# A two-layer trunk step on one core: the end of the first mixer in one written TensorE order, and a constant load later in the queue

## The chip, the core and the metric

The program runs on one core of a Trainium2 chip. The metric is the device time of one execution in microseconds; the median of several runs counts. The engines are TensorE (PE, with its weight loads shown as PEld), VectorE (DVE), ScalarE (ACT), GpSimd (POOL) and SyncE (SP), which here only issues the transfers from and to the device's memory. Each engine works through its own list of instructions in order; semaphores tie the lists together.

## The reference

Two token streams of 128 rows each (a prompt and a sample with cached context) pass through two layers of width 2048. Each layer modulates its input with shift, scale and gate (six vectors from `silu(cond) @ w_ada`), runs a mixer, adds the result, modulates again and runs a gated feed-forward part with a width-3 convolution. The first layer's mixer is the one that the change touches:

```python
def mixer_ab(h, rope, ctx, w_in, g_q, w_q_up, g_kv, w_kv_up, g_qn, g_kn, w_out):
    proj = h @ w_in
    ...
    qa = (rmsnorm(q_lat, g_q) @ w_q_up).reshape(b, t, MLA_HEADS, MLA_NOPE_DIM + MLA_ROPE_DIM)
    ...
    kv = (ckv_all @ w_kv_up).reshape(b, s, MLA_HEADS, MLA_NOPE_DIM + MLA_V_DIM)
    ...
    out_a = softmax_attention(jnp.concatenate([qa_nope, qa_rope], axis=-1), ka, va, MLA_SCALE)
    out_b = softmax_attention(qb, kb_all, vb_all, HEAD_SCALE)
    out = jnp.concatenate([out_a.reshape(b, t, -1), out_b.reshape(b, t, -1)], axis=-1) @ w_out
    return out, new_ctx
```

Eight latent heads (A) and eight grouped heads (B) give 16 x 128 features, and `w_out` (2048 x 2048) projects them.

## The kernel before

Activations lie with features on the 128 partitions: chunk `k` holds features 128k to 128k+127 of the 256 tokens. A matrix product is done in three passes per 128 x 128 block, so that nearly the full precision of 32-bit numbers is kept: each weight tile `raw` is split into a high part `wh` (ScalarE, line 247) and the remainder `wl` (VectorE, line 248), the operand likewise, and TensorE adds wh x high, wh x low and wl x high. A chunk of 128 output features over 16 input blocks is 48 matmuls into one PSUM bank `acc`. The `raw` tiles (1 MB) come over SyncE into three buffers, `wh` and `wl` have four buffers of eight blocks each.

Three kinds of side work run beside these products. `row_step` computes modulation vectors on TensorE from tiles `araw` (tiles `ada`, then a copy `am` on ScalarE, a transpose and a reduction on VectorE). `feature_step` and the class `Deep` compute others on VectorE: line 520 is one such sum of about 1.2 us over half a tile (`block`, `kvb` or `more`, 512 KB, one transfer for two sums), with a product that nobody reads written to a scratch place `junk`. `pump` spreads these steps over the program, and `step` moves on the chains (Python generators) that hold each head's attention.

The first mixer has two parts. In the first, `part` multiplies 23 chunks of `w_in_ab`, in stretches of the input features. Its TensorE order is written out: while `pe.in_turn` is set, each matmul passes `keep_order`, and an instruction that passes it stays behind all that were issued before it on its engine. A class `Feed` sets the order of its transfers; `late_constants` is one of them, 512 KB of constants (rope tables, biases beyond the first, gains) of which VectorE's first use is line 1331.

In the second part, the loop over `h` in 0, 2, 4, 6 makes the queries and keys of two latent heads, begins two grouped heads (`gqa`), makes the values (`values`) and begins the two latent heads (`mla_pair`). Each head goes: scores on TensorE, maxima on VectorE (lines 862 and 863), two small steps on GpSimd, exponentials on ScalarE (line 870), scaling of `p` on VectorE (lines 898 to 900), three transposes on TensorE (line 112, `att<-cst,p`), a copy `pT` on ScalarE, three products with the values, and the split of the result into operand `o` (`hx` in the profile). Chunk `h` of `o` is a latent head, chunk 8 + h a grouped one.

Then `out_ab` multiplies by `w_out`. Its first three chunks go through `first_three`, which names the order of the 48 pairs (chunk c, block k) in `PAIR_LATE`: for each chunk the blocks 8 to 15 (grouped heads), then 0 to 5, last 6 and 7 (the last pair). Here nothing is pinned, apart from one matmul in each pair's scores: a scheduler that works with its own estimates of time places the instructions, and it moves blocks of these three chunks in between the attention of the heads.

## Time and profile before

| | us |
|---|---|
| Median of 3 runs (lowest, highest) | 2307.14 (2306.03, 2307.19) |
| The profiled execution | 2304.7 |
| Its span, first to last instruction | 2302.9 |
| TensorE busy | 2272.1 (99%) |
| VectorE busy | 1886.1 (82%) |
| ScalarE busy | 1199.3 (52%) |
| Mean granted TensorE clock | 0.996 |

Rows of groups and of the timeline give: start in us, duration, engine, source line, operation, output tile <- inputs, shapes and how often; in square brackets the idle time of that engine just before and what ended it. Rows of a stage (a:b) give its length, then busy time (with instructions) of PE, PEld, DVE, ACT and POOL, the granted clock, the share of the transfer engines and GB/s. A matmul's duration in the timeline overlaps its neighbour's, so rates are read from the distance of the starts or from long runs.

### The profile page before, as it was taken

The page shows a single profiled execution, that of the slowest core. Times are in us where ns is not written, and L with a number is a line of the kernel's source. Part 1 is how long each engine was busy: PE and PEld are TensorE (multiplying, and loading weights), DVE is VectorE, ACT ScalarE, POOL GpSimd, SP SyncE. Part 2 cuts the span into 40 slices and gives each one's busy share as a digit, 9 for nine tenths or more (in the row PEclk, how much of TensorE's full clock was granted, in tenths as well). Part 3 has the DMA queues.
Part 4 walks back from the last instruction along what each step waited for, and adds up shares of the span by engine and source line. Part 5 has one row for each costly group of instructions (what it writes and reads, how often), then busy time and mean ns, then how long its engine had stood idle before and what let it go on. Part 6 is the DMA issues. An engine that isn't in the chain of part 4 may idle for free.

```text
span 2302.9 us, 47585 instructions
## 1 busy us (share of the span) xinstructions
PE 2272.1 (99%) x19528; PEld 2180.0 (95%) x19528; DVE 1886.1 (82%) x2973; ACT 1199.3 (52%) x1975; POOL 188.2 (8%) x238
## 2 busy tenths in 40 slices
PE   8899989999999999999999999999999999999998
PEld 6788868999999999999999999999999999999998
DVE  4668979889989999999988988898899965666654
ACT  4346555665554355555575455457555434555543
POOL 0012111300000000001130001023000000000011
PEclk9999999999999999999999999999999999999999
DMA  9988879777767777777787888776677755555553
GB/s 386 374 334 305 329 291 359 290 275 250 272 259 288 286 276 262 260 273 256 284 304 290 311 309 324 259 273 230 245 254 264 263 201 188 199 192 193 198 189 127
DMA packets 100122, 617.15 MB, mean 268 GB/s; under 512 B 10752, under 2 KB 18880, under 8 KB 33344
## 3 DMA queue, kind: packets, MB, share of 16 engines
q1 hardware_dynamic: 99904, 614.11, 72.0%
q8 instruction: 153, 2.51, 0.4%
q14 instruction: 65, 0.53, 0.1%
HBM read 609.32 MB, written 4.75 MB: 267 GB/s over the span
## 4 chain that ended last, share of the span: by engine, by line
PE 96%; DMA 2%; DVE 1%; ACT 1%; issue 0%; SPq 0%; POOL 0%; DVEq 0%; ACTq 0%; POOLq 0%
PE acc L109 89%; PE ada L109 3%; PE att L109 2%; PE att L112 1%; DMA raw<-w_in_ab 1%; DVE wl L248 1%; DMA kvb<-w_ada 0%; DMA araw<-w_ada 0%; PE misc L109 0%; ACT wh L247 0%; PE ada L112 0%; DVE hx L520 0%; DVE x L1616 0%; DVE qb L1138 0%; ACT p L870 0%
## 5 line engine op out<-in xcount | busy, mean ns | idle before, releaser
L109 PE MATMUL acc<-hx,wh 128*128 128x256 f32 (+1 forms) x7264 | 1252.4, 278 | 5.0 <-ACT wh L247 1.7
L247 ACT CAST wh<-raw 128x1024 fp32r<-128x1024 f32 (+1 forms) x834 | 796.6, 967 | 878.8 <-PE acc L109 745.7
L248 DVE TENSOR_TENSOR wl<-raw,wh 128x1024 fp32r<-128x1024 f32 (+1 forms) x834 | 924.4, 1124 | 248.2 <-ACT wh L247 243.3
L109 PEld LDWEIGHTS acc<-hx,wh 128*128 128x128 f32 x7264 | 1097.3, 188 | 23.8 <-issue 8.9
L109 PE MATMUL acc<-hx,wl 128*128 128x256 f32 (+1 forms) x3632 | 1005.7, 277 | 6.3 <-DVE wl L248 6.1
L109 PEld LDWEIGHTS acc<-hx,wl 128*128 128x128 f32 x3632 | 682.9, 188 | 10.5 <-DVE wl L248 7.9
L109 PE MATMUL acc<-g,wh 128*128 128x256 f32 x2816 | 478.8, 276 | 0.0
L109 PEld LDWEIGHTS acc<-g,wh 128*128 128x128 f32 x2816 | 423.8, 188 | 0.0
L109 PE MATMUL acc<-g,wl 128*128 128x256 f32 x1408 | 388.0, 276 | 0.0
L468 DVE CUSTOM_DVE_ANT_0 junk<-araw,condb 128x2048 f32<-128x2048 f32 x128 | 294.1, 2297 | 0.0
L109 PE MATMUL acc<-hxc,wh 128*128 128x256 f32 (+1 forms) x1568 | 282.7, 282 | 0.0
L109 PEld LDWEIGHTS acc<-g,wl 128*128 128x128 f32 x1408 | 264.1, 188 | 0.0
L109 PEld LDWEIGHTS acc<-hxc,wh 128*128 128x128 f32 x1568 | 241.3, 189 | 4.6 <-issue 4.2
L109 PE MATMUL acc<-hxc,wl 128*128 128x256 f32 (+1 forms) x784 | 218.4, 279 | 0.0
L210 POOL TENSOR_TENSOR sqacc<-sqacc,sq 128x256 f32<-128x256 f32 x62 | 71.5, 1154 | 1490.7 <-ACT sq L206 1490.4
L109 PEld LDWEIGHTS acc<-hxc,wl 128*128 128x128 f32 x784 | 147.5, 188 | 0.4
L1509 ACT ACTIVATE cv<-acc,convw 128x256 f32<-128x256 f32 x169 | 94.2, 558 | 0.0
L520 DVE CUSTOM_DVE_ANT_0 hx<-block,condb 128x1024 fp32r<-128x1024 f32 x65 | 79.2, 1218 | 7.4 <-DMA block<-w_ada 6.8
L1515 DVE SCALAR_TENSOR_TENSOR cv<-acc,convw,cv 128x254 f32<-128x254 f32 x169 | 80.8, 478 | 3.2
L838 DVE SCALAR_TENSOR_TENSOR x<-acc,mod,x 128x128 f32<-128x128 f32 x190 | 57.1, 342 | 31.7 <-PE acc L109 31.7
L1512 DVE SCALAR_TENSOR_TENSOR cv<-acc,convw,cv 128x254 f32<-128x254 f32 x169 | 80.1, 474 | 0.0
L109 PE MATMUL ada<-araw,condw 128*32 128x512 f32 (+1 forms) x608 | 75.7, 585 | 0.8 <-DMA araw<-w_ada 0.8
(263 smaller groups left out, 1532.9 us busy)
## 6 DMA issues: line engine op xcount, KB each, us to landing
raw<-w_up SPq DMA_DIRECT2D x176, 1024.0 KB, 4.8
araw<-w_ada SPq DMA_DIRECT2D x136, 1024.0 KB, 6.2
raw<-w_down SPq DMA_DIRECT2D x88, 1024.0 KB, 4.8
raw<-w_in_c SPq DMA_DIRECT2D x48, 1024.0 KB, 6.8
block<-w_ada SPq DMA_DIRECT2D x41, 512.0 KB, 6.6
raw<-w_in_ab SPq DMA_DIRECT2D x18, 1024.0 KB, 9.2
raw<-w_out_ab SPq DMA_DIRECT2D x16, 1024.0 KB, 8.2
raw<-w_out_c SPq DMA_DIRECT2D x16, 1024.0 KB, 6.5
```

Source lines behind the costliest of these rows:

```text
L109: return self.placed(nc.tensor.matmul(*a, **kw))
L112: return self.placed(nc.tensor.transpose(*a, **kw))
L210: eng.tensor_tensor(out=st["acc"], in0=st["acc"], in1=sq, op=ALU.add)
L247: pin(act.copy(out_hi, src))
L248: pin(dve.tensor_tensor(out=out_lo, in0=src, in1=out_hi.bitcast(F32), op=ALU.subtract))
L468: keep_order(dve.tensor_tensor_reduce(out=T_(feat["pool"], [P, D], "junk"), in1=feat["row"][:, c], in0=feat["raw"].rearrange("p g n -> p ( ...
L520: keep_order(dve.tensor_tensor_reduce(out=self.junk, in0=self.raw, in1=self.row[:, c].rearrange("p (g n) -> p g n", g=2), scale=1.0, scala ...
L838: dve.scalar_tensor_tensor(out=x[:, c, s], in0=ps[:, s], scalar=mod[:, l, 3 * which + 2, c, g:g + 1], in1=x[:, c, s], op0=ALU.mult, op1=AL ...
L1509: pin(act.activation(y, ps, AF.Identity, scale=cw[:, 1, m:m + 1], bias=cw[:, 3, m:m + 1]))
L1512: pin(dve.scalar_tensor_tensor(out=y3[:, :, 1:], in0=p3[:, :, :T - 1], scalar=cw[:, 0, m:m + 1], in1=y3[:, :, 1:], op0=ALU.mult, op1=ALU.add))
L1515: pin(dve.scalar_tensor_tensor(out=y3[:, :, :T - 1], in0=p3[:, :, 1:], scalar=cw[:, 2, m:m + 1], in1=y3[:, :, :T - 1], op0=ALU.mult, op1=A ...
```

## The change

`first_three` becomes a class `Three` that can be run in pieces; the function stays as a wrapper for the second mixer. In the loop's last turn (h == 6) the three chunks' weight tiles are requested and two of their halves prepared ahead of the values. From the last pair's scores on, `pe.in_turn` is set until the three chunks end: the scores, 20 blocks of the three chunks (60 matmuls), the transposes of both heads, 4 blocks, the products with the values, and the other 24 blocks. Three calls of `deep.pump` stand between the 20 blocks and one behind the 24th, with `junk` now in `qb`. The weight tile of the fourth chunk is requested there as well, and `out_ab` splits the fourth chunk's weights in two `W.ahead` steps behind the first two residuals. Apart from that, the constants go out behind the first tile of the third weight group (`rest`) instead of behind the second tile of the first one.

```diff
--- before.py
+++ after.py
@@ -329,26 +329,38 @@
             self.blocks = []
             return self.tiles[-1]
 
-    def first_three(W, xh, xl, order, mid=None, fixed=False, first=0):
-
-
-        pin = keep_order if fixed else lambda i: i
-        raws = [W.load()[0] for _ in range(3)]
-        ps = [T_(pacc, [P, 512], "acc") for _ in range(3)]
-        blocks = {(c, h): W.halves(raws[c], 8 * h) for c, h in ((0, first), (1, first), (2, first), (0, 1 - first))}
-        count = [0] * 3
-        for n, (c, k) in enumerate(order):
-            if mid and n == len(order) // 2:
-                mid()
-            if (c, k // 8) not in blocks:
-                blocks[c, k // 8] = W.halves(raws[c], k // 8 * 8)
-            wh, wl = blocks[c, k // 8][k % 8]
-            a, b = count[c] == 0, count[c] == KD - 1
-            count[c] += 1
-            pin(pe.matmul(ps[c][:, :NT], wh, xh(k), start=a, stop=False))
-            pin(pe.matmul(ps[c][:, :NT], wh, xl(k), start=False, stop=False))
-            pin(pe.matmul(ps[c][:, :NT], wl, xh(k), start=False, stop=b))
-        return [p[:, :NT] for p in ps]
+    class Three:
+
+        def __init__(self, W, xh, xl, order):
+            self.W, self.xh, self.xl, self.order = W, xh, xl, list(order)
+            self.raws = [W.load()[0] for _ in range(3)]
+            self.blocks, self.count, self.ps = {}, [0] * 3, []
+
+        def prepare(self, c, h):
+            self.blocks[c, h] = self.W.halves(self.raws[c], 8 * h)
+
+        def banks(self):
+            self.ps = [T_(pacc, [P, 512], "acc")[:, :NT] for _ in range(3)]
+
+        def run(self, n):
+            for _ in range(n):
+                c, k = self.order.pop(0)
+                if (c, k // 8) not in self.blocks:
+                    self.prepare(c, k // 8)
+                wh, wl = self.blocks[c, k // 8][k % 8]
+                a, b = self.count[c] == 0, self.count[c] == KD - 1
+                self.count[c] += 1
+                pe.matmul(self.ps[c], wh, self.xh(k), start=a, stop=False)
+                pe.matmul(self.ps[c], wh, self.xl(k), start=False, stop=False)
+                pe.matmul(self.ps[c], wl, self.xh(k), start=False, stop=b)
+
+    def first_three(W, xh, xl, order):
+        three = Three(W, xh, xl, order)
+        three.banks()
+        for c, h in ((0, 0), (1, 0), (2, 0), (0, 1)):
+            three.prepare(c, h)
+        three.run(len(order))
+        return three.ps
 
     def gemm(blocks, xh, xl, n=NT, first=0, between=None, more=None):
 
@@ -991,7 +1003,6 @@
                 half_load(1, 1)
                 weights(whole)
                 half_load(0, 1)
-                feed.add("late", late_constants)
                 weights(whole)
                 units(2, (0, 1))
                 weights(halves)
@@ -1000,6 +1011,7 @@
                 units(3, (0, 1, 2, 3))
                 weights(halves)
                 weights(rest)
+                feed.add("late", late_constants)
                 for q in (1, 2):
                     for u, ts in ((2 * q + 2, (0, 1)), (2 * q + 2, (2, 3)), (2 * q + 3, (0, 1)), (2 * q + 3, (2, 3))):
                         weights(rest)
@@ -1298,25 +1310,47 @@
                         kn.append(T_(hp, [P, 3 * T], "kn", bufs=2))
                         act.copy(kn[i], ps)
                         pump(RATE["heads"])
-                    mla_pair(h, qr, kn, values())
-                flush()
-
-        return o
-
-    def out_ab(o, st, u, beside, rp):
+                    if h == 6:
+                        W = Weights(A["w_out_ab"], KD, 1)
+                        three = Three(W, lambda k: o[:, k, :NT], lambda k: o[:, k, NT:2 * NT], PAIR_LATE)
+                        three.prepare(0, 1)
+                        three.prepare(1, 1)
+                    vm = values()
+                    pe.in_turn = h == 6
+                    mla_pair(h, qr, kn, vm)
+                deep.junk = qb[:, 0:4].rearrange("p (a b) n -> p a (b n)", a=2)
+                three.banks()
+                step()
+                three.prepare(2, 1)
+                three.prepare(0, 0)
+                for n in (6, 7, 7):
+                    three.run(n)
+                    deep.pump()
+                step()
+                three.run(4)
+                step()
+                deep.pump()
+                W.begun.append(W.load())
+                three.run(len(three.order))
+                pe.in_turn = False
+                assert not chains
+
+        return o, W, three.ps
+
+    def out_ab(o, W, ready, st, u, beside, rp):
         l = 0
         rows = raw_rows(u, l, 1)
         ensure(l, 2)
         ada["pew"] = PEW["out0"]
-        W = Weights(A["w_out_ab"], KD, 1)
         oh, ol = (lambda k: o[:, k, :NT]), (lambda k: o[:, k, NT:2 * NT])
         deep.tiles = [(beside, "block"), (rp, "more")]
         deep.junk = u[:, 14:16, :512]
         deep.rate = SIDE["out0"]
-        ready = first_three(W, oh, ol, PAIR_LATE, first=1)
         for c in range(KD):
             fine[0] = c >= KD - QUIET[1]
             residual(ready.pop(0) if ready else gemm(W.chunk(), oh, ol, first=8), l, 0, c, st)
+            if c < 2:
+                W.ahead(lambda i: i)
             if c == KD - QUIET[1]:
                 deep.flush()
             rows(c)
@@ -1580,11 +1614,11 @@
         hx = operand(keep, "hx")
         st = stat_init()
         with tc.tile_pool(name="beside", bufs=1) as beside:
-            o = mixer_ab(hx, beside)
+            o, *begun = mixer_ab(hx, beside)
             with tc.tile_pool(name="raw", bufs=1) as rp:
                 T_(rp, [P, SHIFT // 4], "pad")
                 u = raw_tile(rp, "u")
-                out_ab(o, st, u, beside, rp)
+                out_ab(o, *begun, st, u, beside, rp)
                 W = Weights(A["w_up"][0], KD, 1)
                 hx, *begun = modulated(st, 0, 1, W, u, (keep, "hx"), rp)
     stage[0] = "ffn0"
```

What the built programs show at three places. First TensorE, from the end of the scores of heads 4 and 5 on (`att_3514`, `att_3515`; `p_3526` and `p_3540` are their softmax). Before:

```order
L109 MATMUL att_3514<-kr_117,qr_3278 128x256
L109 MATMUL att_3515<-kr_117,qr_3278 128x256
L109 MATMUL acc_3947<-hx_2383,wh_3950 128x256 x2
L109 MATMUL acc_3947<-hx_2383,wl_3951 128x256
L109 MATMUL acc_3947<-hx_2383,wh_3950 128x256 x2
```

and the change:

```order
L109 MATMUL att_3514<-kr_117,qr_3278 128x256
L109 MATMUL att_3515<-kr_117,qr_3278 128x256
L112 MATMUL ada_3506<-cst_74,am_3502 128x128 x4
L112 MATMUL att_3607<-cst_74,p_3526 128x128 x3
L112 MATMUL att_3613<-cst_74,p_3540 128x128 x3
L109 MATMUL ada_3623<-araw_3500,condw_79 32x512 x4
L109 MATMUL att_3664<-pT_3611,vm_3426 128x128 x3
```

Before, 54 matmuls of the three chunks (blocks 8 to 13) stand between the scores and the end of the transposes, and 9 more (block 14) in front of the last pair's scores; now all 144 stand behind those scores.

Second VectorE, from the last pair's maxima on (`mx`), up to the scaling of head 6's `p`. Before:

```order
L863 TENSOR_REDUCE mx_3882<-att_3872 128x1
L520 ISA hx_2383,mod_77<-kvb_3868,condb_3299 128x1024
L520 ISA mod_77 128x1
L862 TENSOR_REDUCE mx_3896<-att_3873 128x1
L863 TENSOR_REDUCE mx_3896<-att_3873 128x1
L248 TENSOR_TENSOR wl_4065<-raw_3943,wh_4064 128x512
L520 ISA hx_2383,mod_77<-kvb_3868,condb_3299 128x1024
L520 ISA mod_77 128x1
L248 TENSOR_TENSOR wl_4065<-raw_3943,wh_4064 128x512
```

and the change:

```order
L875 TENSOR_REDUCE mx_3914<-att_3891 128x1
L532 ISA hx_2383,mod_77<-kvb_3886,condb_3299 128x1024
L532 ISA mod_77 128x1
L910 RECIPROCAL rec_3910<-sums_3901 128x2
L532 ISA hx_2383,mod_77<-kvb_3886,condb_3299 128x1024
L532 ISA mod_77 128x1
L532 ISA qb_241,mod_77<-block_3961,condb_3299 128x1024
L532 ISA mod_77 128x1
L911 TENSOR_SCALAR p_3902<-p_3902,rec_3910 128x128
L912 TENSOR_SCALAR p_3902<-p_3902,rec_3910 128x256
```

The maxima now stand together, three feature sums (line 532, formerly 520) come ahead of head 6's scaling, and a pair of weight halves and a fourth sum lie between it and head 7's, which stood together before.

Third ScalarE in the first part, where the copy `am` of modulation sums and the casts of the third weight tile of the first group meet. Before:

```order
L1136 COPY kvb_243<-acc_397 128x256
L398 COPY am_432<-ada_405 128x256
L247 CAST wh_463<-raw_219 128x1024
L247 CAST wh_467<-raw_219 128x768
L1136 COPY kvb_243<-acc_434 128x256
```

and the change:

```order
L1148 COPY kvb_242<-acc_396 128x256
L247 CAST wh_462<-raw_218 128x1024
L247 CAST wh_466<-raw_218 128x768
L410 COPY am_431<-ada_404 128x256
L1148 COPY kvb_242<-acc_433 128x256
```

The casts moved ahead of the copy. VectorE's first use of the late constants (line 1331, now 1365) moved from ahead of that tile's `wl` to the end of the second stretch of the first part.

## The prediction

> **What bounds the kernel now.** I read the page first, then busy time by stage, then TensorE's timeline where it idles.
>
> ```profile
> span 2302.9 us, 47585 instructions
> PE 2272.1 (99%) x19528; PEld 2180.0 (95%) x19528; DVE 1886.1 (82%) x2973; ACT 1199.3 (52%) x1975; POOL 188.2 (8%) x238
> ...
> 0.00:100.00 100.00, 87.23 (x677) 63.79 (x678) 54.13 (x122) 41.27 (x78) 1.41 (x6) 0.97 0.93 375
> 300.00:400.00 100.00, 92.90 (x743) 77.70 (x742) 81.38 (x179) 52.25 (x106) 17.06 (x22) 0.98 0.80 315
> 2000.00:2303.00 303.00, 292.43 (x2578) 292.06 (x2576) 183.12 (x258) 144.29 (x202) 20.64 (x20) 0.98 0.51 181
> ```
>
> TensorE is busy for 2272.1 of 2302.9 us. Of its 30.8 us of idle time, 12.8 lie in the first 100 us, 7.1 between 300 and 400, and 10.6 after 2000, where nothing changes. So the stages that the diff touches hold about 20 us to win, and everywhere else a microsecond lost on TensorE is a microsecond of the whole. The second stretch is the first mixer's end. I cut it at the end of the fourth and fifth head's scores (310.78), at the begin and end of the last pair's scores, and at the last block of the three output chunks (353.05). The columns behind the times are PE, PEld, DVE, ACT and POOL busy, the granted clock, the DMA share and GB/s.
>
> ```profile
> 310.78:335.29 24.51, 19.57 (x150) 14.53 (x149) 18.81 (x51) 11.11 (x28) 4.55 (x8) 0.93 0.80 314
> 335.29:338.01 2.72, 2.72 (x19) 1.76 (x17) 0.54 (x2) 0.37 (x1) 0.00 (x0) 1.00 0.99 408
> 338.01:353.05 15.04, 13.12 (x99) 11.85 (x99) 9.36 (x24) 7.54 (x19) 1.95 (x4) 1.00 0.51 197
> ```
>
> Call them A, B and C: 4.9 us idle in A, none in B, 1.9 in C. The timeline shows what fills A.
>
> ```profile
> 310.15 0.70 PE L109 MATMUL att<-kr,qr 64*128 64x256 f32 x4
> 310.78 0.50 PE L109 MATMUL acc<-hx,wh 128*128 128x256 f32 x2
> ...
> 316.93 0.27 PE L112 MATMUL att<-cst,p 128*128 128x128 f32 x1
> ...
> 328.25 0.87 PE L112 MATMUL att<-cst,p 128*128 128x128 f32 x3 [4.54 <-DVE p L899]
> 329.06 2.97 PE L109 MATMUL ada<-araw,condw 128*32 128x512 f32 x16
> ...
> 335.29 0.61 PE L109 MATMUL att<-kn,qn 128*128 128x128 f32 x4
> ...
> 343.60 0.39 PE L109 MATMUL acc<-hx,wl 128*128 128x256 f32 x1 [1.74 <-DVE wl L248]
> ...
> 348.10 1.15 PE L112 MATMUL att<-cst,p 128*128 128x128 f32 x6
> ```
>
> From 310.78 to 316.93 TensorE does output-projection matmuls while the softmax of heads 4 and 5 runs elsewhere. The softmax of the last two grouped heads has no such filling and costs 4.54 us.
>
> **The written order, stage A.** The new order takes 63 of the 144 matmuls of the three chunks out of A (54 in front of the first transposes, 9 in front of the last scores) and puts them into C. A dense run prices them:
>
> ```profile
> 369.36 16.35 PE acc L109 x144
> ```
>
> 16.35 / 144 = 0.1135 us each, so 63 are 7.15 us. Without them A holds 19.57 - 7.15 = 12.4 us of work. What now stands in the open is the first softmax. Its exponentials and weights are set by ScalarE and VectorE, whose order there stays:
>
> ```profile
> 312.74 1.28 ACT L870 ACT_TABLE_LOAD   x1
> ...
> 315.36 0.29 DVE L899 TENSOR_SCALAR p<-p,rec 128x128 f32<-128x128 f32 x1
> ...
> 316.62 0.29 DVE L899 TENSOR_SCALAR p<-p,rec 128x128 f32<-128x128 f32 x1
> 319.90 1.22 DVE L520 CUSTOM_DVE_ANT_0 hx<-kvb,condb 128x1024 fp32r<-128x1024 f32 x1 [2.74 <-DMA kvb<-w_ada]
> ```
>
> TensorE has one small transpose group left (to 311.15) and then waits for the first p, at 315.65: a new gap of 4.5 us. Behind it come 0.4 us for the second p and, by my estimate, 0.5 for a score bank and a copy. The old gap stays, since VectorE sets it. From the landing at 319.90 VectorE does one feature sum (1.15, from start to start), two low halves (0.7), one pair of maxima (0.65), a sum (1.15), the other maxima (0.55), two sums (2.35) and the scaling of p (0.4), so the transposes start at 326.85 and not 328.25; TensorE is done with its scores at 322.6 and waits 4.3. A becomes 12.4 + 4.5 + 0.9 + 4.3 = 22.1 us, 2.4 less. Least: 1.2 shorter still if the clock stays up after the second gap. B stays 2.7, so the last scores end at 310.8 + 22.1 + 2.7 = 335.6 and not 338.0.
>
> **Stage C.** 60 of the 144 matmuls now stand as one cover behind the scores, 6.8 us, to 342.4. Whether that suffices hangs on VectorE, where the four maxima are followed by feature sums, of which the first waits for a transfer:
>
> ```profile
> 341.18 1.22 DVE L520 CUSTOM_DVE_ANT_0 hx<-kvb,condb 128x1024 fp32r<-128x1024 f32 x1 [2.44 <-DMA kvb<-w_ada]
> ...
> 344.60 1.89 DVE L248 TENSOR_TENSOR wl<-raw,wh 128x512 fp32r<-128x512 f32 x3
> ...
> 331.06 1.38 SPq L578 DMA_DIRECT2D araw<-w_ada  x2
> 332.52 0.38 SPq L517 DMA_DIRECT2D kvb<-w_ada  x1
> ...
> 338.00:339.00 1.00, 1.00 (x11) 1.00 (x10) 0.62 (x2) 0.28 (x1) 0.11 (x1) 1.00 0.91 373
> 339.00:340.00 1.00, 1.00 (x11) 1.00 (x10) 0.00 (x0) 1.00 (x3) 0.30 (x2) 1.00 0.08 33
> ```
>
> Two 1 MB row tiles go out ahead of that tile on SyncE, each when TensorE frees its buffer. They now go 1.75 us sooner (329.2: 326.85, the transposes' 0.87 and half of the 2.97 behind them), so the tile lands at 341.1 - 1.75 = 339.35. The maxima end at 337.0. Then: sum to 340.55, reciprocal and sum to 341.75, a third sum to 342.95, p of head 6 usable at 343.2, a pair of weight halves (1.3) and a fourth sum (1.15) to 346.05, p of head 7 at 346.3. TensorE waits 0.75 for the first and, its transposes being next to each other, 2.5 for the second. So C = 6.8 + 0.75 + 0.57 + 2.5 + 0.57 + 1.36 (12 matmuls) + 1.4 (values) + 8.17 (72 matmuls) = 22.1, 7.1 us more. Bounds for the landing: the bulk moves by the row of 338 to 339 some 2 us before the old landing, so it may be 337.4, and C is then 20.0; a landing 1 us later makes it 23.1. With no wait at all C is 18.9.
>
> Gaps also cost clock:
>
> ```profile
> 328.00:329.00 1.00, 0.74 (x3) 0.48 (x3) 0.73 (x4) 0.57 (x3) 0.00 (x0) 0.50 0.70 246
> 330.00:331.00 1.00, 1.00 (x12) 0.31 (x8) 0.96 (x3) 0.00 (x0) 0.00 (x0) 0.50 0.02 8
> ```
>
> After the 4.54 us gap the granted clock is 0.50 for some 3 us, about 1.6 us lost. A has that already. Behind the new first gap, half speed falls on work that waits for VectorE anyway: nothing. Behind the last wait, 3.25 us in two pieces, it would fall on work that counts: between 0 and 1.6, I take 0.8, as the gap lies between 4.54 and the 1.74 us one at 341.9 to 343.6, after which the clock stays 1.00 (the row of stage C).
>
> [...]
>
> **Weights for the next chunk** are begun earlier; its start loses about 0.3 us on weight halves today: -0.3. The three extra feature-sum steps and their transfers only move forward from the output projection, where TensorE has no idle time. The two projection tiles that go out later on SyncE serve chunks 4 and 5, needed after 365: hidden.
>
> **The constants.** 512 KB leave a queue that is full from 8 to 80 us, and ScalarE's order follows:
>
> ```profile
> 8.00:80.00 72.00, 62.40 (x516) 45.96 (x514) 40.14 (x99) 31.95 (x67) 0.70 (x1) 0.95 1.00 409
> ...
> 21.98 0.43 SPq L152 DMA_DIRECT2D cst<-cst  x1
> 22.46 1.57 SPq L273 DMA_DIRECT2D raw<-w_in_ab  x1
> ...
> 37.33 0.16 DVE L1331 TENSOR_TENSOR shift<-cst 128x2 f32<-128x2 f32 x1 [0.63 <-DMA cst<-cst]
> ...
> 40.77 0.37 ACT L398 COPY am<-ada 128x256 f32<-128x256 f32 x1 [1.58 <-PE ada L109]
> 41.04 1.78 ACT L247 CAST wh<-raw 128x1024 fp32r<-128x1024 f32 x2
> ...
> 43.41 0.38 PE L109 MATMUL acc<-hx,wl 128*128 128x256 f32 x1 [0.74 <-DVE wl L248]
> ```
>
> The weight tile behind the constants lands 1.3 us sooner (0.52 MB at 409 GB/s), its two casts go ahead of the copy `am`, which waits for TensorE, and the 0.74 us wait goes: -0.7. It can be -1.5 if a later wait shortens with it, and up to +0.7 if the constants, now sent near 59, land after VectorE's use of them near 73 (the old landing took 15.3 us, which would be 74).
>
> **Sum.** -0.7 - 2.4 + 7.1 + 0.8 - 0.3 = +4.5 us. The profiled execution took 2304.7 with a span of 2302.9, the median of the runs is 2307.14: so a span near 2307.4 and a median of **2311.6 us**, 0.2% slower. From no change a measurement here tells about 0.2%, 4.6 us.
>
> **Rivals.** *The gaps run on at half clock.* If the last wait lasts to a landing 1 us later and the clock then halves fully (+1.0 + 0.8), and the constants give nothing (+0.7): +7.0, 2314.1. For it: 0.50 in the only long gap. Against: 1.00 behind the shorter one.
>
> *The cover nearly suffices.* If the tile lands at 337.4, or the sums slip behind the scaling, C is 20.0 and the clock holds: -0.7 - 2.4 + 5.0 - 0.3 = +1.6, 2308.7. The three such tiles between 300 and 350 us took:
>
> ```profile
> DMA to landing us min/median/max: 5.6/8.6/11.2
> ```
>
> For it speaks the 5.6, against it that the tile in this very place took 8.6.
>
> *The start gives it all back, and the kernel is not slower.* From 44 to 90 us TensorE idles for another 46.0 - 39.0 = 7.0 us:
>
> ```profile
> 44.00:90.00 46.00, 39.02 (x320) 30.63 (x322) 32.93 (x77) 18.70 (x35) 0.00 (x0) 1.00 0.94 383
> ...
> 71.52 0.50 PE L109 MATMUL acc<-hx,wh 128*128 128x256 f32 x2 [1.71 <-ACT wh L247]
> ```
>
> If all of it hung on the full DMA queue and went, the sum would be 4.5 - 7.0 = -2.5, 2304.6; it decides from 4.5 of the 7.0. Against: the longest wait names ScalarE's weight cast, not a transfer, and the share of the queue is as full afterwards, since the constants only move back in it.
>
> **Numbers.** Forecast 0.50 (its own range 2309.5 to 2313), half clock 0.20, near cover 0.22, start 0.08. Half of the forecast and nearly all of the half-clock case pass 4.6 us: slower 0.48, within 0.2% 0.47, faster 0.05. Range 2307.0 to 2315.0: it takes in both neighbours and leaves out the start.
>
> **What would show it.** A gap of 4 to 5 us before the transposes of heads 4 and 5; a second one of about 4.3; last scores some 2 us earlier; 1 to 3 us of wait between the transposes of heads 6 and 7, named VectorE's p, with a feature sum waiting for its tile; the last block of the three chunks 4 to 5 us later, less the start's gain; no wait at 43. Wrong it would be if the first gap were missing, or if the last p came before 342.4.

## The result and the profile after

| | before | after |
|---|---|---|
| Median of the runs made side by side, us (lowest, highest) | 2307.16 (2304.61, 2310.01), 6 runs | 2316.28 (2315.49, 2318.72), 6 runs |
| Ratio, 95% interval | | 1.0040 [1.0030, 1.0051] |
| The profiled execution, us | 2304.7 | 2315.71 |
| Its span | 2302.9 | 2313.9 |

The change makes the kernel 9.1 us slower, where 4.5 was forecast, and its median lies above the range, which ended at 2315.0. The two profiled executions stand 11.0 us apart; the difference of 1.9 is that the one of before was the quickest of its six runs, 2.5 us below their median. The lines named here stand 12 further down in the changed kernel: L899 of before is L911 of after, L642 is L654, L520 is L532.

The page of after begins so:

```profile
span 2313.9 us, 47587 instructions
...
PE 2277.6 (98%) x19528; PEld 2183.8 (94%) x19528; DVE 1887.8 (82%) x2975; ACT 1199.6 (52%) x1977; POOL 188.8 (8%) x238
```

Busy time by stretch, and by the stages A, B and C of the prediction (columns as there):

```profile
100.00:200.00 100.00, 97.23 (x807) 82.23 (x806) 67.82 (x130) 46.98 (x80) 11.49 (x14) 1.00 0.83 323
...
300.00:400.00 100.00, 88.63 (x666) 71.63 (x665) 80.75 (x185) 51.30 (x112) 17.84 (x23) 0.93 0.79 305
...
314.55:338.89 24.34, 15.91 (x87) 8.31 (x85) 17.95 (x47) 11.20 (x28) 6.25 (x8) 0.79 0.81 309
338.89:341.61 2.72, 2.72 (x19) 1.76 (x17) 1.29 (x6) 0.37 (x1) 0.00 (x0) 1.00 0.80 268
341.61:365.10 23.49, 20.68 (x164) 20.06 (x163) 16.48 (x40) 8.77 (x24) 0.82 (x4) 0.93 0.61 221
```

TensorE is idle for 11.4 us between 300 and 400 (7.1 before), and for 2.8 between 100 and 200, where before it had no gap at all. Heads 4 and 5's scores already end at 314.55 and not at 310.78: 3.8 us are lost before the mixer's end begins. Stage A, which I expected 2.4 us shorter, is as long as before (24.34, before 24.51). B is the same. C takes 23.49 where it took 15.04. TensorE's timeline names the waits:

```profile
125.75 0.39 PE L109 MATMUL acc<-hx,wh 128*128 128x256 f32 x1 [1.97 <-DVE hx L654]
...
178.81 0.39 PE L109 MATMUL acc<-hx,wl 128*128 128x256 f32 x1 [0.64 <-DVE wl L248]
...
319.46 0.95 PE L112 MATMUL att<-cst,p 128*128 128x128 f32 x3 [4.25 <-DVE p L911]
320.91 0.87 PE L112 MATMUL att<-cst,p 128*128 128x128 f32 x3 [0.51 <-DVE p L911]
...
323.58 2.62 PE L109 MATMUL att<-pT,vm 128*128 128x128 f32 x12
...
332.20 0.71 PE L112 MATMUL att<-cst,p 128*128 128x128 f32 x3 [3.48 <-DVE p L911]
...
349.18 0.61 PE L112 MATMUL att<-cst,p 128*128 128x128 f32 x3 [0.55 <-DVE p L911]
352.05 0.61 PE L112 MATMUL att<-cst,p 128*128 128x128 f32 x3 [2.26 <-DVE p L911]
...
354.59 2.40 PE L109 MATMUL att<-pT,vm 128*128 128x128 f32 x12
```

The five waits on p are the forecast ones (4.5, 0.4, 4.3, 0.75 and 2.5 us in the prediction). The first two rows are not. And twice the products of a pair with its values (`att<-pT,vm`) take 2.4 to 2.6 us, 1.60 in the same place before: they run at half clock, 0.50 in the one-us windows behind the two gaps (the seventh column is PE's clock).

```profile
322.00:323.00 1.00, 1.00 (x8) 0.00 (x0) 0.00 (x0) 0.36 (x1) 0.00 (x0) 0.50 0.79 324
...
354.00:355.00 1.00, 1.00 (x6) 1.00 (x6) 0.51 (x2) 0.38 (x1) 0.00 (x0) 0.50 0.86 320
```

What VectorE does between 119 and 126 explains the first row. Before (first fence) it finishes the operand rows of the third quarter (`nt`, then `hx`) with one weight half between them; after (second fence) a weight half stands ahead of `nt` and another ahead of the second `hx`.

```profile
119.27 1.12 DVE L653 TENSOR_SCALAR nt<-nt,scl,mod 128x128 f32<-128x128 f32 x4
120.30 1.22 DVE L248 TENSOR_TENSOR wl<-raw,wh 128x1024 fp32r<-128x1024 f32 x1
...
121.76 0.86 DVE L642 TENSOR_TENSOR hx<-nt,hx 128x256 fp32r<-128x256 f32 x1
...
122.88 0.63 DVE L642 TENSOR_TENSOR hx<-nt,hx 128x256 fp32r<-128x256 f32 x1
```

```profile
119.28 1.23 DVE L248 TENSOR_TENSOR wl<-raw,wh 128x1024 fp32r<-128x1024 f32 x1
120.42 1.11 DVE L665 TENSOR_SCALAR nt<-nt,scl,mod 128x128 f32<-128x128 f32 x4
...
121.78 0.90 DVE L654 TENSOR_TENSOR hx<-nt,hx 128x256 fp32r<-128x256 f32 x1
...
123.59 1.44 DVE L248 TENSOR_TENSOR wl<-raw,wh 128x1024 fp32r<-128x1024 f32 x1
...
125.28 0.41 DVE L654 TENSOR_TENSOR hx<-nt,hx 128x256 fp32r<-128x256 f32 x1
```

The second `hx` comes at 125.28 and not at 122.88, and TensorE waits for it. Nothing in the diff speaks of these instructions: the scheduler has sorted the first part's lists anew, because a load that it takes into account moved. The runs below test this. My theory after the result: the change has two prices, a new list in the start (by the load), and the mixer's end (by gaps, half clock and VectorE's order ahead of the last p).

### The profile page after: what moved, and what is told of

Its sections match the earlier page's. It is cut to its first block, busy times and chain, and to the rows that moved or that the text cites. A ratio compares the mean times of both kernels' runs of the same rounds, so it can differ in the third digit from the quotient of the medians.

```text
span 2313.9 us, 47587 instructions
## 1 busy us (share of the span) xinstructions
PE 2277.6 (98%) x19528; PEld 2183.8 (94%) x19528; DVE 1887.8 (82%) x2975; ACT 1199.6 (52%) x1977; POOL 188.8 (8%) x238
## 4 chain that ended last, share of the span: by engine, by line
PE 95%; DVE 2%; DMA 2%; ACT 1%; issue 0%; SPq 0%; POOL 0%; DVEq 0%; ACTq 0%
PE acc L109 88%; PE ada L109 3%; PE att L109 2%; PE att L112 1%; DVE wl L248 1%; DMA kvb<-w_ada 1%; DMA raw<-w_in_ab 1%; DMA araw<-w_ada 0%; PE misc L109 0%; PE ada L112 0%; ACT wh L247 0%; DVE hx L532 0%; DVE x L1650 0%; DVE hx L693 0%; DVE qb L1150 0%
## 5 line engine op out<-in xcount | busy, mean ns | idle before, releaser
L532 DVE CUSTOM_DVE_ANT_0 hx<-block,condb 128x1024 fp32r<-128x1024 f32 x64 | 78.2, 1221 | 5.8 <-DMA block<-w_ada 5.2
```

Source lines behind the costliest of these rows:

```text
L532: keep_order(dve.tensor_tensor_reduce(out=self.junk, in0=self.raw, in1=self.row[:, c].rearrange("p (g n) -> p g n", g=2), scale=1.0, scala ...
```

## The experiments

Each was timed beside the kernel before on one chip. A ratio is to that kernel, with its 95% interval.

| run | median, us | before, us | ratio [interval] |
|---|---|---|---|
| e1_const | 2308.89 | 2306.93 | 1.0008 [0.9999, 1.0017] |
| e2_const_early | 2305.66 | 2306.93 | 0.9993 [0.9984, 1.0002] |
| e3_mixer | 2310.69 | 2306.93 | 1.0015 [1.0006, 1.0024] |
| e4_both_early | 2309.94 | 2306.93 | 1.0013 [1.0004, 1.0022] |
| e5_sums_late | 2313.89 | 2307.51 | 1.0032 [1.0021, 1.0043] |
| e6_clock | 2314.13 | 2307.51 | 1.0028 [1.0018, 1.0039] |
| e7_fill | 2303.60 | 2307.51 | 0.9983 [0.9974, 0.9992] |
| e8_sums_early | 2309.69 | 2307.51 | 1.0010 [1.0001, 1.0019] |
| e9_const_next | 2306.39 | 2306.75 | 0.9999 [0.9990, 1.0008] |
| e10_fill_cover | 2301.08 | 2306.75 | 0.9974 [0.9963, 0.9985] |
| e11_fill_sums | 2302.93 | 2306.75 | 0.9983 [0.9974, 0.9993] |
| e12_fill_old_const | 2301.96 | 2306.77 | 0.9977 [0.9968, 0.9986] |

### The two parts alone

e1 is the kernel before with the load moved as in the change:

```diff
                 half_load(0, 1)
-                feed.add("late", late_constants)
                 weights(whole)
...
                 weights(rest)
+                feed.add("late", late_constants)
                 for q in (1, 2):
```

> The kernel before with the constants' load moved as in the change, nothing else. Its lists of VectorE and ScalarE up to the mixer's end are those of the change (weight halves of coming chunks ahead of operand rows of the third quarter). Theory (the list that the scheduler sorts anew costs the start): heads 4 and 5's scores end near 314.5 us (310.78 before, 314.55 with the change), with a wait of 1.5 to 2.5 us of TensorE on VectorE's hx near 125; the whole run 3 to 4 us above the kernel before. Rival (the start's loss was a difference between two executions, or comes with the written order): scores end at 310 to 311.5, the run within 1 us of before.

e2 moves it less far:

```diff
                 half_load(0, 1)
-                feed.add("late", late_constants)
                 weights(whole)
...
                 units(3, (0, 1, 2, 3))
+                feed.add("late", late_constants)
                 weights(halves)
```

> The kernel before with the constants' load moved less far: behind the four tiles of the fourth row unit, still 10 transfers later than before and outside the first weight tiles. Here the lists of VectorE and ScalarE stay as before, apart from the constants' own first use and one weight half. Theory (the list costs, not the transfer): no wait near 125, scores of heads 4 and 5 end at 310 to 311, the wait of 0.74 us near 43 gone, the run between 1 us below and 0.5 above the kernel before. Rival (the later transfer itself costs, by the queue): as with the full move, 3 to 4 us above.

e3 is the change without the moved load:

```diff
                 half_load(0, 1)
+                feed.add("late", late_constants)
                 weights(whole)
...
                 weights(rest)
-                feed.add("late", late_constants)
                 for q in (1, 2):
```

> The change with the constants' load put back to its old place: the mixer's end alone. Theory (the two parts add up): scores of heads 4 and 5 end near 310.8 as before; from there to the last block of the three chunks 50 to 51 us instead of 42.3, so 8 us more, of which about 1 is regained later: 6.5 to 8 us above the kernel before. Rival (the written order also makes the start slower): scores end near 314, the run 9 us above. My own forecast for this part alone was 5.2 (+4.5 with 0.7 from the constants).

e4 is the change with the load at e2's place:

```diff
                 units(3, (0, 1, 2, 3))
+                feed.add("late", late_constants)
                 weights(halves)
                 weights(rest)
-                feed.add("late", late_constants)
```

> The change with the constants' load at the place of the run that moves them less far, so that the start's lists stay as before. Theory: 3 to 4 us below the change, within 1 us of the mixer's end alone (6.5 to 8 us above the kernel before). Rival (the later transfer itself costs): the change's own time, 9 us above.

The start can be measured between four landmarks on TensorE, the first modulation product (`ada<-araw`) near 89, 130, 178 and 193 us (starts, from the timeline). Ahead of 89 the executions differ whatever the load's place: two waits near 71 us (1.7 to 1.8 and 0.76) were followed by half clock in those of after, e5, e6, e7, e8 and e11 and not in those of before, e9 and e10. e7, e8, e10 and e11 have the load at one place, and their first landmarks are 89.75, 90.00, 87.28 and 89.43.

| | 89 to 130 | 130 to 178 | 178 to 193 |
|---|---|---|---|
| before | 40.94 | 47.51 | 14.38 |
| after | 43.31 | 48.18 | 15.16 |
| e1: load moved as in the change | 45.04 | 48.05 | 15.16 |
| e2: load moved less far | 40.95 | 47.51 | 14.38 |
| e3: load at its old place | 41.28 | 47.38 | 14.38 |
| e4: mixer's end, load as in e2 | 41.01 | 47.51 | 14.38 |
| e9: load moved by one place | 41.05 | 48.17 | 15.16 |

Only the kernels with the new lists are late, with and without the written order, so the loss behind 89 is the load's and not a difference between executions. The second and the third stretch belong together: in the new lists six small products (`misc`, sums of squares) lie behind the third landmark and not ahead of it, and the third stretch has no wait. Together the two take 61.89 us before and in e2, and 63.34 in after, of which TensorE is idle for 0.8. The wait of 0.74 us near 43, which I had counted as the whole effect, is gone in e1 and in e2, and e2 lies 1.3 us below the kernel before (1 was the most expected, and its interval still reaches no change). e1's whole, 2.0 us above before, is less than the 3 to 4 that I expected, and its interval reaches from no change to 3.9. e1's 45.04 is 1.7 above the change's own figure, although the lists are the same: the same wait of 1.97 us was followed by 3.42 us at half clock there and by full clock in the change (last section).

```profile
125.23 0.39 PE L109 MATMUL acc<-hx,wh 128*128 128x256 f32 x1 [1.97 <-DVE hx L642]
```

e4 was expected 3 to 4 us below the change and lies 6.3 below; beside the kernel before the two cost 0.9 to 5.1 and 6.9 to 11.8 us by their intervals, and they differ in the load's place alone. e3 costs 3.8 us, where I expected 6.5 to 8, and e1 2.0, together 5.8 and not 9.1. So some 3 us seem to come only where both are present. The intervals of e1 and e3 (1.4 to 5.5) hardly tell that from none, but the traces show 2.9 us of it at the mixer's end (second part of the next table).

### Does the list decide, or how far the load moves?

e9 moves the load by one place:

```diff
-                feed.add("late", late_constants)
                 weights(whole)
+                feed.add("late", late_constants)
                 units(2, (0, 1))
```

> The kernel before with the constants' load moved by one place only: behind the weight tile that followed it. The scheduler sorts anew here as well, but only partly: VectorE's rows for the third quarter's operands stay as before, the list of the last stretch (the queries' rows among the products) is that of the full move. Theory (the list that the scheduler happens to make sets the start's price, not how far the load moves): from the fourth-unit products at 88 to those at 130 41 us, as before, no wait on hx near 125; from 177 to 192 15.2 us, as with the full move, against 14.4 before; the run 0 to 1.5 us above the kernel before. Rival (the price grows with the distance of the move): both stretches as before, the run within 0.5 us of before or below.

The table above has its row. The third quarter's list is as before and so is its time (41.05); the last stretch's list is that of the full move, and its time is 15.16 to the hundredth. With the second stretch it makes 63.33 us, as in after (63.34). TensorE's landmarks before (first fence) and in e9 (second):

```profile
177.31 1.92 PE L109 MATMUL ada<-araw,condw 128*32 128x512 f32 x16
...
191.69 1.90 PE L109 MATMUL ada<-araw,condw 128*32 128x512 f32 x10
```

```profile
178.22 1.92 PE L109 MATMUL ada<-araw,condw 128*32 128x512 f32 x16
...
193.38 1.90 PE L109 MATMUL ada<-araw,condw 128*32 128x512 f32 x10
```

A move by one place costs the last two stretches together 1.4 us, one by six places (e2) nothing. So in these traces the list decides, not the distance. The whole missed: it is 0.4 us below before, where I expected 0 to 1.5 above and the rival less than 0.5; its interval, from 2.3 below to 1.8 above, can't tell the two.

### The mixer's end

e5 issues the feature sums behind the blocks:

```diff
                 for n in (6, 7, 7):
                     three.run(n)
-                    deep.pump()
                 step()
                 three.run(4)
                 step()
-                deep.pump()
                 W.begun.append(W.load())
                 three.run(len(three.order))
                 pe.in_turn = False
+                for n in range(4):
+                    deep.pump()
```

> The change with one edit: the four calls that issue feature sums between and behind the 20 blocks now stand behind the last block of the three chunks. TensorE's, ScalarE's lists stay; on VectorE the scaling of p of heads 6 and 7 moves ahead of two sums. Theory (the order on VectorE sets the last waits): the wait of 0.55 us before head 6's transposes goes, that of 2.26 falls below 0.7, the values of heads 6 and 7 run at full clock (1.5 us instead of 2.40), so from the last pair's first score to the first modulation product behind the chunks 22 to 23 us instead of 26.2; the run 3 to 4.5 us below the change (2316.3). Rival (the landing of the kvb tile sets both): the waits stay within 0.5 us, the run within 1 us of the change.

e6 fills the first gap with work that nobody needs:

```diff
                     vm = values()
+                    if h == 6:
+                        spare_bank = T_(pacc, [P, 512], "acc")[:, :NT]
+                        with tc.issue_after(pair_score[0].ins):
+                            for n in range(36):
+                                wh, wl = three.blocks[n // 18, 1][n // 3 % 6]
+                                pe.matmul(spare_bank, wh, o[:, 8 + n // 3 % 6, :NT], start=True, stop=True)
                     pe.in_turn = h == 6
```

> The change with 36 more matmuls in the first gap: behind the scores of heads 4 and 5, into a spare bank that nobody reads, 4.1 us of work for TensorE that the result does not need. Theory (half clock behind the first gap took the gain that I had forecast for stage A): granted clock 1.00 from 318 to 325, the values of heads 4 and 5 take 1.6 us and not 2.62, the last pair's first score comes 1.5 to 2.5 us after less (stage A 22 to 23 us instead of 24.3) although TensorE does more. Rival (VectorE sets the end of stage A alone, by its sums and the kvb tile): stage A 24 us or more, with a longer second gap. The whole run is not a test here, since VectorE's list behind it is sorted anew too.

e8 is e5's edit on e4.

> The same edit as in the run that moves the sums, but with the constants at the place that keeps the start's lists. Theory: here VectorE already scaled p between the sums (waits 0 and 1.06), so the edit brings at most 1 us: 2309 to 2310, still 2 to 3 us above the kernel before, which is the price of the written order alone: the first gap and its half clock. Rival (the sums are the whole price): within 1 us of the run with the constants alone at this place, 2305.7.

The mixer's end in two parts of the profiled executions, us: from the first score of heads 4 and 5 to the first of the last pair (stage A with 2.8 us of scores), and from there to the first modulation product behind the blocks (B and C).

| | first part | second part |
|---|---|---|
| before | 27.27 | 17.80 |
| after | 27.10 | 26.21 |
| e3 | 25.99 | 23.28 |
| e4 | 27.21 | 22.55 |
| e5 | 27.38 | 21.85 |
| e6 | 25.08 | 21.91 |
| e8 | 27.80 | 22.24 |

*The 3 us of the second part.* e4 has the change's TensorE and ScalarE orders there, and is 3.7 us shorter. VectorE's order is what differs; the tile itself comes 3.4 us behind the last scores in e4 and 3.6 in the change. In the change it waits 2.32 us for the `kvb` tile, and three sums (line 532) stand ahead of head 6's p (line 911) and a fourth ahead of head 7's; in e4 (second fence) it waits 0.69 us, one sum stands ahead of head 6's p and two more ahead of head 7's.

```profile
345.19 1.23 DVE L532 CUSTOM_DVE_ANT_0 hx<-kvb,condb 128x1024 fp32r<-128x1024 f32 x1 [2.32 <-DMA kvb<-w_ada]
...
346.46 1.22 DVE L532 CUSTOM_DVE_ANT_0 hx<-kvb,condb 128x1024 fp32r<-128x1024 f32 x1
...
347.61 1.22 DVE L532 CUSTOM_DVE_ANT_0 qb<-block,condb 128x1024 f32<-128x1024 f32 x1
...
348.75 0.28 DVE L911 TENSOR_SCALAR p<-p,rec 128x128 f32<-128x128 f32 x1
...
350.48 1.22 DVE L532 CUSTOM_DVE_ANT_0 qb<-block,condb 128x1024 f32<-128x1024 f32 x1
...
351.62 0.28 DVE L911 TENSOR_SCALAR p<-p,rec 128x128 f32<-128x128 f32 x1
```

```profile
342.12 1.23 DVE L532 CUSTOM_DVE_ANT_0 hx<-kvb,condb 128x1024 fp32r<-128x1024 f32 x1 [0.69 <-DMA kvb<-w_ada]
...
343.27 0.28 DVE L911 TENSOR_SCALAR p<-p,rec 128x128 f32<-128x128 f32 x1
...
343.81 1.20 DVE L532 CUSTOM_DVE_ANT_0 hx<-kvb,condb 128x1024 fp32r<-128x1024 f32 x1
...
344.94 1.22 DVE L532 CUSTOM_DVE_ANT_0 qb<-block,condb 128x1024 f32<-128x1024 f32 x1
...
346.69 0.28 DVE L911 TENSOR_SCALAR p<-p,rec 128x128 f32<-128x128 f32 x1
```

e5 shows it by an edit: with the sums behind, both waits go, the values take 1.50 us, and the second part falls by 4.36. Of these 2.7 are idle time (0.1 us is left of 2.8) and 1.65 busy time (21.75 for 23.40 by the windows of this part), the price of half clock behind the waits. The whole gains only 2.4 of the 3 to 4.5 expected, since VectorE is now late in the output projection (0.50 us on x at 363.22, and this):

```profile
389.77 0.38 PE L109 MATMUL acc<-hx,wl 128*128 128x256 f32 x1 [1.11 <-DVE wl L248]
```

e8's median is 0.25 us below e4's, as expected: where VectorE's list was kind already, the sums cost next to nothing.

*Half clock in the first part.* In the change the clock stays at half for 6.84 us behind the first gap (the first row shows six of these). e6 does 4.1 us more matmuls and is 2.0 us shorter there, at full clock behind that gap (second row):

```profile
319.00:325.00 6.00, 5.04 (x20) 2.58 (x21) 2.69 (x10) 2.05 (x6) 0.12 (x1) 0.50 0.74 273
```

```profile
318.00:321.00 3.00, 3.00 (x28) 2.78 (x25) 2.17 (x6) 3.00 (x4) 1.48 (x2) 1.00 1.02 426
```

```profile
326.04 1.60 PE L109 MATMUL att<-pT,vm 128*128 128x128 f32 x12
...
333.63 0.87 PE L112 MATMUL att<-cst,p 128*128 128x128 f32 x3 [3.48 <-DVE p L911]
```

The values take 1.60 us and not 2.62, and the second gap is the same 3.48: its p comes that much sooner, since VectorE's chain starts from the values' result. From the split of the second head's result to that p it is 5.1 us in the change (p at 331.77, first row) and in e6 (p at 333.20, second row):

```profile
326.65 0.42 DVE L248 TENSOR_TENSOR hx<-att,hx 128x256 fp32r<-128x256 f32 x1 [0.55 <-ACT hx L247]
```

```profile
328.09 0.42 DVE L248 TENSOR_TENSOR hx<-att,hx 128x256 fp32r<-128x256 f32 x1 [0.25 <-ACT hx L247]
```

The rival, that VectorE alone sets the end of A, falls. e4, e5 and e8, which have the first gap too, agree: the longer the values take at half clock, the longer the first part, 2.62 us and 27.10 in the change, 2.66 and 27.21 in e4, 2.88 and 27.38 in e5, 2.93 and 27.80 in e8. e6's whole is no test, as expected, since VectorE's list behind is another one (its second part, without a wait, is 4.3 us shorter than the change's).

### A version from it

e7 takes e2's place for the load, e5's place for the sums, and deals the blocks out by hand:

```diff
                     vm = values()
+                    if h == 6:
+                        three.banks()
+                        three.prepare(2, 1)
+                        three.prepare(0, 0)
+                        three.run(12)
+                        with tc.issue_after(last_score[0].ins):
+                            three.run(12)
+                        pe.in_turn = True
+                        for _ in range(3):
+                            step()
                     mla_pair(h, qr, kn, vm)
...
                 step()
+                three.run(15)
+                step()
+                three.run(3)
+                step()
```

The transposes of the last two grouped heads wait three steps more to be issued, and the blocks come in this order: 8 to 13 of the three chunks, 0 to 5 of the first, 14 and 15, then the others. A pin (`keep_order`) would not do: by the built lists, which are not printed here, it holds an instruction behind the one issued just before it on its engine, not behind all that were, as the description of the kernel above has it. `issue_after` names the instruction.

> A version that uses what the runs showed: constants at the place that keeps the start's lists, feature sums behind the three chunks, and the 48 blocks dealt out by hand: 12 into the gap behind the scores of heads 4 and 5, 12 into the gap behind the scores of the last two grouped heads, 18 behind the last pair's scores, 6 at the end. Theory (the waits of the mixer's end are TensorE work that stands in the wrong place): no gap over 1.5 us between the scores of heads 4 and 5 and the last block, clock 1.00 throughout, so the mixer's end is 3 to 6 us shorter than in the kernel before, and the run 3 to 7 us below it (2300 to 2304). Rival (VectorE and ScalarE, which must prepare the same weights and softmax, set the end): waits come back on wl or p, the run within 2 us of the kernel before.

It is 3.9 us faster than the kernel before. Its mixer's end, though, is only 1.0 us shorter in the profiled executions (44.1 for 45.1), and not 3 to 6; where the rest comes from is open. The two long gaps are gone; 0.57 (on wl), 1.38 and 1.05 us (on p) remain behind the last scores, and the values there run at half clock (2.29 us), where I expected full clock throughout. e10 moves four blocks there from the second gap, where TensorE came too late:

```diff
-                            three.run(12)
+                            three.run(8)
...
-                three.run(15)
+                three.run(19)
```

> The hand-dealt version with four blocks taken from the second gap (where TensorE came 1.5 us late to p) and put behind the last pair's scores, 22 blocks instead of 18. Theory (the cover behind the last scores was too short by the waits of 0.57, 1.38 and 1.05): these waits fall below 1 us together and the values of heads 6 and 7 run at full clock, 1.5 us for 2.29; the run 1 to 3 us below the first such version (2303.6). Rival (VectorE, with weight halves and sums ahead of p, moves the p as far back as the cover grows): waits of 2 us or more, the run within 1 us of it.

e11 also holds back the sums that the last values issue:

```diff
-                            pump(RATE["heads"])
+                            pump(RATE["heads"], beside=not last)
...
-                for n in range(4):
+                for n in range(6):
                     deep.pump()
```

> As the run before it, and in addition the last values issue no feature sums; they follow behind the three chunks. On VectorE two sums fewer stand between the last maxima and the scaling of p. Theory: no wait over 0.5 us at p of heads 6 and 7; the run 0.5 to 2 us below the version that keeps these sums. Rival (the sums only move to the output projection, where VectorE is then late): the gain at p is given back, the run within 0.5 us of it or above.

e12 is e10 with the load at its old place.

> The hand-dealt version with 22 blocks behind the last scores, with the constants' load back at its old place; all lists but for one row stay. Theory (the constants at their list-keeping place bring the 0.7 us wait near 43 and nothing more): the run 0.5 to 1.5 us above the version with the moved load (2301.1), so still 4 to 5 us below the kernel before. Rival (the moved load is a main part of that version's gain): 3 us or more above it.

e10 is 5.7 us faster than the kernel before (e7 3.9), and so some 15 faster than the change. In its stretch from 300 to 400 the clock is whole, the last values take 1.50 us, and TensorE idles for 4.0 us:

```profile
300.00:400.00 100.00, 95.98 (x773) 80.60 (x772) 85.49 (x190) 54.09 (x111) 18.56 (x23) 1.00 0.88 333
```

```profile
338.76 0.39 PE L110 MATMUL acc<-hx,wl 128*128 128x256 f32 x1 [1.12 <-DVE wl L249]
...
342.70 0.44 PE L113 MATMUL att<-cst,p 128*128 128x128 f32 x2 [0.38 <-DVE p L915]
```

The wait on p is down to 0.38, but that on wl grew to 1.12, so they are 1.5 together and not below 1. e11 missed: its waits on p are gone, and it is 1.9 us slower than e10 (their intervals overlap). The rival fits: in the profiled executions the second part is 1.9 us shorter than e10's, and the stretch from there to the modulation product near 440 is 2.0 longer. Most of that is not VectorE, which the rival named, but TensorE's wait for ScalarE's squares at the end of the output projection:

```profile
433.10 0.38 PE L110 MATMUL att<-cst,sq 128*128 128x1 f32 x2 [1.66 <-ACT sq L207]
```

e12 is 0.9 above e10, as expected and within what the intervals leave open: the moved load is at most a small part of the gain, where it leaves the lists alone.

## Why the prediction was wrong, point by point

In the profiled executions the sum reads: start +3.8, A -0.2, B 0, C +8.5, the next chunk -0.2 (7.70 us between the modulation products on both sides of it, 7.91 before), behind it -0.8, which no run separates; together 11.0.

**The constants, -0.7: the step that failed.** The one wait that I looked at went as said. But I priced the moved load by the weight tile behind it alone, and took the lists up to 310 as they stood apart from one cast. They were sorted anew, and rows of operands lost their place to weight halves of later chunks. The three stretches lose 2.4 + 0.7 + 0.8 us: 2.0 of it is the wait on `hx` near 125, 0.8 are waits in the second (0.64 of it on `wl`), and the rest is TensorE's own work in another order, whose cause stays open. By the medians the load alone cost 2.0 (e1). My bounds, -1.5 to +0.7, came from waits between 41 and 74 us, where the load was and where it went, and the price lay between 118 and 193. The new list at the mixer's end, also by the load, is in stage C, which I had forecast from the order of the changed kernel itself.

**Stage A, -2.4: half clock priced at nothing.** The gaps came as forecast, if shorter: 4.25 us for 4.5, 0.51 behind it, 3.48 for 4.3. TensorE's work between them took 15.9 us for 12.4. What failed is the sentence that half speed behind the first gap falls on work that waits for VectorE anyway. It falls on the values of heads 4 and 5, and VectorE waits for these; and it lasted 6.84 us where the gap of the kernel before had 3.4. By e6 that is 2.0 us of the 2.2 missing.

**Stage B, 2.7:** 2.72.

**Stage C, 22.1, and 0.8 for the clock:** 23.49, with waits of 0.55 and 2.26 for 0.75 and 2.5. The tile came 3.6 us behind the last scores (345.19 against 341.61) where I had 3.75 (339.35 against 335.6). The clock's term is the upper end of its bounds: 3.42 us at half clock behind the wait of 2.26, 1.65 by e5, for 0.8.

**The next chunk's weights, -0.3:** -0.2.

**The rivals.** The nearest was "the gaps run on at half clock" with 2314.1. Of its three conditions one came, the full half clock behind the last wait; the landing was not later, and the start did not just give nothing but lost time. It was still 2.2 us short, for a cause that no case held. "The cover nearly suffices" is what e4 did by its list (0 and 1.06 us of wait). The start gave nothing back.

The order of the waits at the mixer's end was right, and e3, which is that part alone, cost 3.8 us for the 5.2 of its terms: its first part is 1.3 us shorter than before and not 2.4, its second 5.5 longer and not 7.9.

## What to carry to other kernels

Where a scheduler sorts the lists, a moved load can be a change to every list behind it: compare the lists of all engines to the end of the program, and price the rows that other engines wait for. Of places that serve equally, take one that leaves the lists alone. The first gap was paid twice here, by its length (4.25 us) and by the 6.84 us at half clock behind it, worth 2.0 by e6, since VectorE waited for the values that ran there; work that can stand anywhere is best dealt into each gap in the measure of that gap.

## What the runs showed of the hardware

A wait of TensorE of 2.0 us at one place (near 125) was followed by half clock in two of four profiled executions and by full clock in the other two: 1.97 with it in e1 and without in after, 2.06 with it in e6 and without in e5. In e7 two waits of 1.38 and 1.05 with 0.6 us of matmuls between were followed by it. Waits of 1.74 (before, near 343), 1.53 (e3) and 1.06 (e4) at the mixer's end were not. In e1's one-us windows the clocks of 0.60, 0.50, 0.50 and 0.69 add up to 3.42 us at half speed (0.80 + 1 + 1 + 0.62); in after, behind the gap of 2.26, the windows from 353 to 357 (0.53, 0.50, 0.50, 0.76) give the same 3.42. Counted so, the stretches at half speed up to 460 us come to 3.42, 3.42 and 3.40 us in before and to 6.82, 3.42, 6.84, 3.42 and 3.42 in after. The same gap was not followed by the same time at half speed: behind 4.54 us the sixteen modulation products took 2.97 us in before and 3.64 in e9, where those ahead of it took 1.92 in both.

```profile
126.00:127.00 1.00, 1.00 (x8) 1.00 (x8) 1.00 (x3) 0.00 (x0) 0.00 (x0) 0.60 1.05 442
127.00:128.00 1.00, 1.00 (x6) 1.00 (x6) 0.31 (x1) 0.00 (x0) 0.00 (x0) 0.50 0.53 221
128.00:129.00 1.00, 1.00 (x7) 1.00 (x6) 0.42 (x1) 0.74 (x1) 0.00 (x0) 0.50 0.25 107
129.00:130.00 1.00, 1.00 (x8) 1.00 (x7) 0.00 (x0) 0.31 (x1) 0.00 (x0) 0.69 0.06 25
```
